# Other places for retention's first tiles, attention values copied out of PSUM, later sigmoids and weight splits, result sums in pieces

## The chip, the cores and the metric

The kernel runs on one NeuronCore of a Trainium2 chip. TensorE (PE) multiplies matrices and writes PSUM, VectorE (DVE), ScalarE (ACT) and GpSimd (POOL) work on tiles, and DMA queues move data between the chip's memory and the on-chip SBUF. SyncE (SP) issues most of the DMAs, GpSimd a few. Every engine works through its own instructions in the order in which they stand, and waits where an operand or the place of a result is not free. The metric is the device time of one execution in microseconds. Lower is better.

## The reference, cut to what matters

One decoder block on a sequence of 1024 tokens with 1024 channels, all in float32. The change touches the two token mixers that run in parallel, retention and dilated attention, and the gates that merge them.

```python
def step(state, inp):              # retention: 4 heads, dk 256, dv 512, 8 chunks of 128
    qi, ki, vi = inp
    s = einsum('bhid,bhjd->bhij', qi, ki) * inner_decay
    o = einsum('bhij,bhje->bhie', s, vi) + einsum('bhid,bhde->bhie', qi, state) * q_decay
    state = state * chunk_decay + einsum('bhjd,bhje->bhde', ki * k_decay, vi)
    return state, o

# token_mixer, after proj = h @ w_in and its split into parts
ro = group_norm(retention(rotary(rq), rotary(rk) * dk ** -0.5, rv))
ret_out = (silu(rg) * ro) @ w_ret_out
for gi, (win, dil) in enumerate(((128, 1), (512, 4), (2048, 16))):   # 4 heads of 128 in each
    o, lse = dilated_group(aq, ak, av, bias, win, dil)   # softmax over a band of keys
att = sum over groups of softmax(lse over groups) * o
att_out = att @ w_att_out
merged = sigmoid(gate_a) * ret_out + sigmoid(gate_b) * att_out
return merged @ w_o
```

Around it stand the modulation by `silu(c) @ w_ada` and the squared-ReLU MLP.

## The kernel before, in words

Float32 products are made of three matmuls on rounded parts: each operand is split into a high part (a cast on ScalarE) and a low part (a subtraction on VectorE), and `mm3` (L197) multiplies low by high, high by low and high by high. A raw weight block of 128x1024 comes in by a DMA on SP's queue and is split by `split_w` (L188). The stages stand in one list of steps. `Steps.run` (L72 to L132) issues the raw loads a few ahead, splits the weights that a step needs, and by default splits those of the next two steps before the body of the step; a step marked manual gets a function `ahead` and calls it where it likes. The order of the work on each engine is the order in which the code issues it; there is no planner. Tiles come from pools in which a new tile waits for the last use of whatever lay in its place.

Values stage (L1072 to L1105): retention's values are projected, modified and stored to the chip's memory in pieces (`vd<-vo`, `vd<-vr`). Then `open_ret` (L517) opens retention's pool over the memory of this stage. Its first tiles are the state and its two parts, and then come the tiles of the chunks.

Retention (`chunk`, L675 to L743): 32 steps g, four heads of eight chunks. A step issues part of the gate projection (rg), the product of keys and values (kv, two halves in two PSUM banks), the scores and key transposes of the next step (`s_kt`: sT, then sm, smh and sml by ScalarE and VectorE, kT, then kh and kl), the state update, the output (o: queries by state, scores by values), the split of the state (stateh, statel), the split of the queries of step g + 2 (`jit_qk`, L608: j, high part on ScalarE and low part on GpSimd), the group norm of o, and the transposes of the last one (`on_T`, L652). `fetch` (L586) brings queries, keys and values three steps ahead. Every step also prepares one modulation block (raw, L455). `u_final` (L663) stores the results of a head (y) to memory.

Result sums (`result_sums`, L574): four blocks of y are added pairwise to t1 to t4 in memory, each by a copying and an adding DMA on GpSimd's queue over all heads. They are issued in the first attention step and are read in the retention output stage (`r_x_load`, L1630).

Attention: two pairs of heads. For each pair `att_step` (L1472) projects keys (ak) and makes scores (sc) and exponentials for six combinations of group and head. Then `cover_step` (L1507 to L1540) runs four gate projections, numbered 0 to 3, in whose course the softmax weights are made (`weights`, L1333), the probabilities are scaled (`pscale`, L1362) and the products with the values are woven in: `pv_tr` (L1380) transposes a bank of probabilities and splits it (pth, ptl), `pv_mm` (L1392) multiplies it by the values (pv), and `pv_end` (L1412) takes the sum out of PSUM: a ScalarE copy for group 0, a VectorE addition to the sum P for groups 1 and 2, and at the end the split of the head's output (ah, al). `v_fetch` and `v_split` (L1291, L1295) bring and split the values (vh, vl). Each gate goes through a sigmoid out of PSUM (L1538) and is stored. Group 2's products run in the step that follows: in the first attention step of the second pair, or for the last pair in `gate_step` (L1557), after which the attention output is projected (ao, `att_out_step`).

## Time and profile before

| | us |
|---|---|
| median of 3 runs | 2228.99 |
| lowest, highest | 2226.23, 2230.13 |
| profiled execution, its own time | 2226.56 |
| its span, first to last instruction | 2224.8 |
| TensorE busy | 2177.1 (98% of the span) |
| VectorE busy | 1454.5 (65%) |
| ScalarE busy | 907.3 (41%) |
| GpSimd busy | 145.5 (7%) |
| mean granted TensorE clock | 0.997 |

Retention's first step stands at about 660 us in the span, the first attention step at about 985, the first pair's cover steps from about 1065, the second pair's from about 1225. A row of a timeline gives start, duration, engine, line, operation, result <- operands, shape, and in brackets the engine's idle time before it with what released it. The granted clock is a share of TensorE's full clock. An average over the span says little here: what a change in one stage is worth is read from that stage's rows.

### The profile page before, as it was taken

Reading aid. Unit: us, or ns where it says so; the run is one execution under the profiler, and the core shown is the slowest. Engines: PE = TensorE matmul, PEld = TensorE weight load, DVE = VectorE, ACT = ScalarE, POOL = GpSimd, SP = SyncE. Lnnn points to the kernel's source line nnn. Section 1 sums busy time; section 2 is a strip of 40 time slices with the busy share of each in tenths; the row PEclk is TensorE's granted clock in tenths of the full one; section 3 lists DMA queues with packets and bytes.
Section 4 is the critical chain, followed back from the end, with each engine's and each line's share of the span. In section 5 each row is a group of like instructions: output and inputs, shape, how many; then the busy total and the mean of one; then the engine's idle time right before and its main releaser. Section 6 shows DMA issues by size and latency. Waiting matters only on the chain.

```text
span 2224.8 us, 27161 instructions
## 1 busy us (share of the span) xinstructions
PE 2177.1 (98%) x10130; PEld 1803.4 (81%) x10130; DVE 1454.5 (65%) x2285; ACT 907.3 (41%) x1665; POOL 145.5 (7%) x168
## 2 busy tenths in 40 slices
PE   7999999999999999999999999999999999999998
PEld 4888888888877888888888788888778888888887
DVE  6628777764448778855554644676876665787855
ACT  4323332223434445544534633424454445533412
POOL 0001111000012122100000000002100000000003
PEclk9999999999999999999999999999999999999999
DMA  9539999725775556549813355645144444745322
GB/s 364 200 134 284 299 284 284 200 103 189 250 268 169 167 179 212 188 162 248 235 60 96 105 196 211 237 160 176 62 149 152 149 156 168 261 139 171 122 85 77
DMA packets 154371, 408.93 MB, mean 184 GB/s; under 512 B 27062, under 2 KB 54973, under 8 KB 149822
## 3 DMA queue, kind: packets, MB, share of 16 engines
q1 hardware_dynamic: 148542, 363.14, 46.5%
q0 software_dynamic: 5696, 44.04, 8.4%
q8 instruction: 80, 1.31, 0.2%
q14 instruction: 53, 0.43, 0.1%
HBM read 316.27 MB, written 156.13 MB: 212 GB/s over the span
## 4 chain that ended last, share of the span: by engine, by line
PE 86%; DVE 6%; ACT 3%; DMA 2%; issue 1%; POOL 0%; SPq 0%; POOLq 0%; DVEq 0%; ACTq 0%
PE qap L203 5%; PE qap L201 5%; PE qap L205 5%; PE av L769 4%; PE fp L203 4%; PE fp L201 4%; PE fp L205 4%; PE rg L201 2%; PE rg L203 2%; PE rg L205 2%; PE f2a L203 2%; PE f2a L201 2%; PE f2a L205 2%; PE ak L201 2%; PE ak L203 2%; PE ak L205 2%
## 5 line engine op out<-in xcount | busy, mean ns | idle before, releaser
L201 PE MATMUL qap<-hh,qaw 128*128 128x512 f32 x216 | 84.0, 389 | 0.0
L203 PE MATMUL qap<-hl,qaw 128*128 128x512 f32 x216 | 84.0, 389 | 0.0
L205 PE MATMUL qap<-hh,qaw 128*128 128x512 f32 x216 | 84.0, 389 | 0.0
L616 POOL TENSOR_TENSOR j<-qk,j 128x512 fp32r<-128x512 f32 x32 | 43.3, 1352 | 465.0 <-ACT j L615 465.0
L1918 ACT ACTIVATE a<-a 128x512 f32<-128x512 f32 x48 | 30.3, 632 | 76.2 <-DVE a L1917 76.2
L1272 ACT ACTIVATE P<-P,ng 128x128 f32<-128x128 f32 (+1 forms) x96 | 41.9, 438 | 39.2 <-DVE ng L1269 39.2
L258 DVE TENSOR_TENSOR fw<-w1r,fw 128x512 fp32r<-128x512 f32 x48 | 33.0, 688 | 37.6 <-ACT fw L248 37.6
L1815 POOL TENSOR_TENSOR accnf<-accnf,sqnf 128x256 f32<-128x256 f32 (+1 forms) x18 | 16.6, 922 | 613.5 <-ACT sqnf L1814 613.4
L258 DVE TENSOR_TENSOR qaw<-wa,qaw 128x512 fp32r<-128x512 f32 x54 | 36.0, 685 | 30.9 <-ACT qaw L248 30.9
L2104 ACT CAST w2h<-w2s 128x512 fp32r<-128x512 f32 x36 | 22.4, 621 | 78.1 <-DVE w2s L2142 77.0
L201 PE MATMUL fp<-h2h,fw 128*128 128x512 f32 x128 | 50.0, 390 | 0.0
L203 PE MATMUL fp<-h2l,fw 128*128 128x512 f32 x128 | 49.8, 389 | 0.0
L205 PE MATMUL fp<-h2h,fw 128*128 128x512 f32 x128 | 49.8, 389 | 0.0
L201 PE MATMUL roa<-rh,rwl 128*128 128x512 f32 x128 | 49.8, 389 | 0.0
L203 PE MATMUL roa<-rl,rwh 128*128 128x512 f32 x128 | 49.8, 389 | 0.0
L205 PE MATMUL roa<-rh,rwh 128*128 128x512 f32 x128 | 49.8, 389 | 0.0
L1653 DVE TENSOR_TENSOR rwl<-rwl,rwh 128x1024 fp32r<-128x1024 f32 x25 | 30.2, 1221 | 29.1 <-ACT rwh L1683 29.1
L638 ACT COPY sm<-sT 128x128 f32<-128x128 f32 x32 | 8.5, 266 | 98.8 <-PE sT L629 92.7
L201 PEld LDWEIGHTS qap<-hh,qaw 128*128 128x128 f32 x216 | 40.5, 188 | 8.5
L205 PEld LDWEIGHTS qap<-hh,qaw 128*128 128x128 f32 x216 | 40.5, 188 | 8.4
L203 PEld LDWEIGHTS qap<-hl,qaw 128*128 128x128 f32 x216 | 40.5, 188 | 8.4
L1815 POOL TENSOR_TENSOR accn<-accn,sqn 128x512 f32<-128x512 f32 x12 | 15.5, 1294 | 478.5 <-ACT sqn L1814 478.5
(3081 smaller groups left out, 7181.0 us busy)
## 6 DMA issues: line engine op xcount, KB each, us to landing
v<-vd SPq DMA_DIRECT2D x32, 512.0 KB, 4.9
raw<-in_w_ada_dram SPq DMA_DIRECT2D x32, 512.0 KB, 4.9
w1r<-in_w_ff_dram SPq DMA_DIRECT2D x32, 512.0 KB, 5.0
vd<-vo SPq DMA_DIRECT2D x24, 512.0 KB, 6.5
yt<-y POOLq DMA_DIRECT2D x6, 2048.0 KB, 15.3
xsd<-as SPq DMA_DIRECT2D x24, 512.0 KB, 2.7
w2r<-in_w_ff2s_dram SPq DMA_DIRECT2D x24, 512.0 KB, 7.6
em<-in_w_ada_dram SPq DMA_DIRECT2D x16, 512.0 KB, 10.2
```

The lines of the kernel that those rows point to most:

```text
L201: nc.tensor.matmul(o, wl, xh, start=first, stop=False, skip_group_check=skip)
L203: nc.tensor.matmul(o, wh, xl, start=False, stop=False, skip_group_check=skip)
L205: nc.tensor.matmul(o, wh, xh, start=False, stop=last, skip_group_check=skip)
L258: nc.vector.tensor_sub(t[:, 512:], src, fv(t[:, :512]))
L616: nc.gpsimd.tensor_sub(t[:, 1], src, fv(t[:, 0]))
L638: nc.scalar.copy(sm, ps[:, :C])
L769: nc.tensor.matmul(av[g][c], x[k][:, c * C:(c + 1) * C], w[j][:, ws], start=k == 0 and (x, j) == parts[0], stop=k == NK - 1 and (x, j) == ...
L1272: nc.scalar.activation(v, v, AF.Exp, bias=ng[:, blk:blk + 1], accum_out=st[:, g, blk, 2 + a:3 + a])
L1653: nc.vector.tensor_sub(lo, fv(lo), fv(hi))
L1815: (nc.vector if f == 7 else nc.gpsimd).tensor_add(G["acc", key], G["acc", key], sq)
L1918: nc.scalar.activation(o, o, AF.Relu)
L2104: nc.scalar.copy(hi, src)
```

## The change: what it does

1. Retention's start. The first split query tile j2, the score tiles and the key tiles of step 0 are allocated first in retention's pool (`chunk_tiles`), the state tiles last, after the fetches for steps 1 and 2 have been issued. In step 0 the state's parts are taken straight out of PSUM, the plain state is copied by ScalarE later, j2 is split before the output instead of after it, and the modulation blocks of steps 0 and 1 are both prepared ahead of step 0.
2. Weights in attention. A step marked "late" gets the preparation of the following two steps as a function and calls it inside its body (`following`).
3. Attention's cover steps. Gates 0 to 2 are copied out of PSUM in halves by VectorE and ScalarE; their sigmoids run in SBUF later, among the value products. `pv_end` copies every product out of PSUM on ScalarE and adds from SBUF. The values of the first group are fetched a step earlier, their high parts are cast before the weights and their low parts taken inside `weights`.
4. Result sums. y and t1 to t4 are tensors for each head, and the sums are 32 transfers of a quarter of the size, issued two in each projection of the attention stage (`with_sums`) and the rest ahead of `gate_step`.

On TensorE the same instructions stand in the same order. VectorE has 5 more, ScalarE 17, GpSimd 24 more (DMA issues); SP's queue has as many, in another order.

```diff
                 issue()
+        def following(s, mine):
+            room = 3 - max(mine, 1)
+            for t in (s + 1, s + 2):
+                if t < len(self.steps) and self.steps[t][2] is True and not self.steps[t][0]:
+                    break
+                if t < len(self.steps) and room > 0:
+                    done = sum(getattr(p, "weight", False) for _, p in self.steps[t][0][:len(results[t])])
+                    prepare(t, room - done, t == s + 2)
+                    room -= weights_of(t)
+                    if len(results[t]) < len(self.steps[t][0]):
+                        break
         pre(issue, lambda room: prepare(0, room), self.marks + [len(flat)])
...
             args = [r for r in results[s] if r is not None]
-            if manual:
+            if manual == "late":
+                body(lambda s=s, mine=mine: following(s, mine), *args)
+            elif manual:
                 body(lambda room=3 - mine, only=False: prepare(s + 1, room, only), *args)
             else:
...
+                following(s, mine)
                 body(*args)
...
         R["p"] = ret_ctx.enter_context(tc.tile_pool(name="ret", bufs=1, reuse_waits="tile"))
-        R["state"] = R["p"].tile([P, 2, DV], F32, name="state")
-        R["sh"] = R["p"].tile([P, 2, DV], F32R, name="stateh")
-        R["sl"] = R["p"].tile([P, 2, DV], F32R, name="statel")
     def etile(name, dt=F32):
         return R["p"].tile([P, 1024], dt, tag="E", bufs=12, name=name)
-    y_d = dram.tile([P, 4, 8, 512], F32, name="y")
-    yt_d = {n: dram.tile([P, 8, 512], F32, name=f"y{n}") for n in ("t1", "t2", "t3", "t4")}
+    y_d = [dram.tile([P, 4, 2, 512], F32, name=f"y{h}") for h in range(H)]
+    yt_d = {n: [dram.tile([P, 2, 512], F32, name=f"y{n}{h}") for h in range(H)] for n in ("t1", "t2", "t3", "t4")}
     YB = ("11", "12", "21", "22")
...
         add(s4, src[1, j])
-    def dma_sum(out, x, y):
...
     def gn_signs():
...
-    def result_sums():
...
+    def sums_of(h):
+        b11, b12, b21, b22 = (y_d[h][:, i] for i in range(4))
+        t1, t2, t3, t4 = (yt_d[n][h] for n in ("t1", "t2", "t3", "t4"))
+        return [(t1, b11, 0), (t1, b12, 1), (t2, t1, 0), (t2, b22, 1), (t4, t2, 0), (t4, b21, 1), (t3, b12, 0),
+                (t3, b22, 1)]
+    sums_left = []
+    def result_sum():
+        if sums_left:
+            out, x, add = sums_left.pop(0)
+            out, x = (t.rearrange("p a b -> p (a b)") for t in (out, x))
+            if add:
+                nc.gpsimd.dma_start(out, x, accum_op=ALU.add, max_dma_last_dim=8192)
+            else:
+                nc.gpsimd.dma_start(out, x)
+    def with_sums(gen):
+        return at(at(gen, 1, result_sum), 5, result_sum)
     hd = {}
...
         if i > 1:
-            t = R["p"].tile([P, 2, 4, C], F32R, tag="j", bufs=2, name=f"j{i}")
+            t = R.pop("j", None)
+            if t is None:
+                t = R["p"].tile([P, 2, 4, C], F32R, tag="j", bufs=2, name=f"j{i}")
         else:
...
         hd["j", i] = t
+    def chunk_tiles():
+        p = R["p"]
+        R["j"] = p.tile([P, 2, 4, C], F32R, tag="j", bufs=2, name="j2")
+        R["sm"] = p.tile([P, C], F32, tag="sm", bufs=1, name="sm00")
+        for n in ("smh", "sml"):
+            R[n] = p.tile([P, C], F32R, tag=n, bufs=2, name=n + "00")
+        for n in ("kh", "kl"):
+            R[n] = p.tile([P, 2, P], F32R, tag=n, bufs=1, name=n + "00")
     def s_kt(i):
...
                 nc.tensor.transpose(pk[:, i, :], hd["qk", g][:, 2 + i], ident)
-        sm = p.tile([P, C], F32, tag="sm", bufs=1, name=f"sm{h}{c}")
-        smh = p.tile([P, C], F32R, tag="smh", bufs=2, name=f"smh{h}{c}")
-        sml = p.tile([P, C], F32R, tag="sml", bufs=2, name=f"sml{h}{c}")
+        if g == 0:
+            sm, smh, sml = R["sm"], R["smh"], R["sml"]
+        else:
+            sm = p.tile([P, C], F32, tag="sm", bufs=1, name=f"sm{h}{c}")
+            smh = p.tile([P, C], F32R, tag="smh", bufs=2, name=f"smh{h}{c}")
+            sml = p.tile([P, C], F32R, tag="sml", bufs=2, name=f"sml{h}{c}")
         nc.scalar.copy(sm, ps[:, :C])
...
             kd = ct[:, CS_KDEC + h:CS_KDEC + h + 1]
-            kh = p.tile([P, 2, P], F32R, tag="kh", bufs=1, name=f"kh{h}{c}")
-            kl = p.tile([P, 2, P], F32R, tag="kl", bufs=1, name=f"kl{h}{c}")
+            if g == 0:
+                kh, kl = R["kh"], R["kl"]
+            else:
+                kh = p.tile([P, 2, P], F32R, tag="kh", bufs=1, name=f"kh{h}{c}")
+                kl = p.tile([P, 2, P], F32R, tag="kl", bufs=1, name=f"kl{h}{c}")
             nc.scalar.mul(kh, pk, kd)
...
             nc.vector.tensor_mul(t, t, hd["srg", h, e])
-            nc.sync.dma_start(y_d[:, 2 * (i % 2):2 * (i % 2) + 2, i // 2], t.rearrange("p (t x) -> p t x", t=2))
+            nc.sync.dma_start(y_d[h][:, 2 * (i % 2):2 * (i % 2) + 2, e // 2], t.rearrange("p (t x) -> p t x", t=2))
     def chunk(h, c, ahead, w=None):
...
         for i, kv in enumerate(kvs):
-            if c == 0:
+            if g == 0:
+                nc.scalar.copy(sh[:, i, :], kv)
+                nc.vector.tensor_sub(sl[:, i, :], kv, fv(sh[:, i, :]))
+            elif c == 0:
                 nc.vector.tensor_copy(st[:, i, :], kv)
...
                                                op0=ALU.mult, op1=ALU.add)
-        if g > 0:
-            ahead(2)
+        if g == 0:
+            jit_qk(2)
+        ahead(2)
         if 0 < g < NG - 1:
...
         mm3([po], hd["s", g], [(vh, vl)], c == 0, True)
-        if c < NC - 1:
+        for i in range(2) if g == 0 else ():
+            nc.scalar.copy(st[:, i, :], kvs[i])
+        if g > 0 and c < NC - 1:
             for i in range(2):
...
                 nc.vector.tensor_sub(sl[:, i, :], st[:, i, :], fv(sh[:, i, :]))
-        if g + 2 < NG:
+        if 0 < g < NG - 2:
             jit_qk(g + 2)
...
         hd["o", h, c] = on
-        if g == 0:
-            ahead(2)
         if c % 2 == 1:
...
         open_ret()
+        chunk_tiles()
         for g in (1, 2):
             fetch(g)
+        R["state"] = R["p"].tile([P, 2, DV], F32, name="state")
+        R["sh"] = R["p"].tile([P, 2, DV], F32R, name="stateh")
+        R["sl"] = R["p"].tile([P, 2, DV], F32R, name="statel")
         banks(False)
...
             steps.add((lambda h, c: lambda ahead, *w: chunk(h, c, ahead, *w))(h, c),
-                      ([wsplit(io["w_rg"][4 * h + c // 2])] if c % 2 == 0 else []) + [mod_load(later_mods[8 * h + c])],
+                      ([wsplit(io["w_rg"][4 * h + c // 2])] if c % 2 == 0 else []) +
+                      [mod_load(later_mods[8 * h + i]) for i in ({0: (0, 1), 1: ()}.get(8 * h + c, (c,)))],
                       manual=True)
...
             nc.sync.dma_start(fv(lo).rearrange("p (a b) -> p a b", a=4), v_rows(pair, g, j))
-    def v_split(pair, g):
+    def v_split(pair, g, low=True):
         for j in range(2):
...
             nc.scalar.copy(hi, fv(lo))
-            nc.vector.tensor_sub(lo, fv(lo), fv(hi))
             A["v", g, j] = (hi, lo)
+            if low:
+                v_low_part(g, j)
+    def v_low_part(g, j):
+        hi, lo = A["v", g, j]
+        nc.vector.tensor_sub(lo, fv(lo), fv(hi))
     def vblk(g, blk, a, i):
...
         nc.scalar.activation(wt, wt, AF.Exp)
+        for j in range(2):
+            v_low_part(0, j)
         for g in range(3):
...
         else:
+            t = A["P", g, a][:, :1024]
+            nc.scalar.copy(t, f)
             r = 4 * g
             sv = sumt.rearrange("p (i r) -> p r i", r=r)
-            nc.vector.tensor_add(sv, f.rearrange("p (r i) -> p r i", r=r), sv)
+            nc.vector.tensor_add(sv, t.rearrange("p (r i) -> p r i", r=r), sv)
         if g == 2:
...
             ps = ps_mm(f"ak{pair}{i}")
-            gen = proj_gen(ps, args[-1])
-            if i == len(combos) - 1:
+            gen = with_sums(proj_gen(ps, args[-1]))
+            if i == len(combos) - 2:
                 v_fetch(pair, 0)
...
                 u_final(H - 1)
-                result_sums()
+                for h in range(H):
+                    sums_left.extend(sums_of(h))
                 open_att()
...
             else:
-                weave_pv(at(gen, 0, lambda: v_split(0, 2)), NK - 1, 0, 2)
+                weave_pv(at(at(gen, 0, lambda: v_split(0, 2)), 5, args[0]), NK - 1, 0, 2)
             if i == 0:
...
             ps = ps_mm(f"gate0{i}")
-            gen = proj_gen(ps, args[-1])
+            gen = with_sums(proj_gen(ps, args[-1]))
             if n == 0:
...
                 drain(gen)
+                v_split(pair, 0, False)
                 scores_end(pair, *combos[-1])
...
             elif n == 1:
-                drain(at(gen, 4, lambda: v_split(pair, 0)))
+                drain(gen)
             elif n == 2:
                 v_fetch(pair, 2)
-                gen = at(gen, 3, lambda: (args[0](3), v_split(pair, 1)))
+                gen = at(at(gen, 3, lambda: (args[0](3), v_split(pair, 1))), 5, sigmoids)
                 weave_pv(gen, NK - 1, pair, 0)
...
             else:
-                weave_pv(at(gen, 3, lambda: [pscale(2, a) for a in range(2)]), NK - 1, pair, 1)
+                gen = at(at(at(gen, 3, lambda: [pscale(2, a) for a in range(2)]), 5, args[0]), 6, sigmoids)
+                weave_pv(gen, NK - 1, pair, 1)
             if n > 1:
...
                 t = ring(f"g0{i}s", F32)
-            nc.scalar.activation(t, flat(ps), AF.Sigmoid)
+            if n < 3:
+                nc.vector.tensor_copy(t[:, :512], ps[:, 0])
+                nc.scalar.copy(t[:, 512:], ps[:, 1])
+                raw_gates.append((i, t))
+            else:
+                nc.scalar.activation(t, flat(ps), AF.Sigmoid)
+                nc.sync.dma_start(gate_d[i], t)
+        return body
+    raw_gates = []
+    def sigmoids():
+        while raw_gates:
+            i, t = raw_gates.pop(0)
+            nc.scalar.activation(t, t, AF.Sigmoid)
             nc.sync.dma_start(gate_d[i], t)
-        return body
     for pair in range(2):
...
                       ([(aq_d[pair, *combos[i - 1]], q_prep(pair, *combos[i - 1]))] if i > 0 else []),
-                      manual=i == pair == 0)
+                      manual=("late" if pair else True) if i == 0 else False)
         for n in range(len(COVER[pair])):
             more = [(aq_d[pair, *combos[-1]], q_prep(pair, *combos[-1]))] if n == 0 else []
-            steps.add(cover_step(pair, n), more + [wsplit(io["w_gate"][len(COVER[0]) * pair + n])], manual=n == 2)
+            steps.add(cover_step(pair, n), more + [wsplit(io["w_gate"][len(COVER[0]) * pair + n])], manual={2: True, 3: "late"}.get(n, False))
     G = {}
...
     mh_ctx = ExitStack()
-    def gate_step(w):
+    def gate_step(ahead, w):
+        while sums_left:
+            result_sum()
         ps = ps_mm("gate9")
         gen = at(proj_gen(ps, w), 2, lambda: v_split(1, 2))
-        gen = at(gen, 3, lambda: [pscale(2, a) for a in range(2)])
-        weave_pv(gen, NK - 1, 1, 1, 2)
+        gen = at(at(gen, 3, lambda: [pscale(2, a) for a in range(2)]), 5, ahead)
+        weave_pv(at(gen, 4, sigmoids), NK - 1, 1, 1, 2)
         att_ctx.close()
...
         nc.sync.dma_start(G[b, j], gate_d[8 * b + j])
-    steps.add(gate_step, [wsplit(io["w_gate"][len(COVER[0] + COVER[1])])])
+    steps.add(gate_step, [wsplit(io["w_gate"][len(COVER[0] + COVER[1])])], manual="late")
     def open_mh():
...
         b = RPLAN[n][0]
-        src = y_d[:, YB.index(b)] if b in YB else yt_d[b]
         for m in range(4):
+            h = 2 * c + m // 2
+            src = y_d[h][:, YB.index(b)] if b in YB else yt_d[b][h]
             Q["x", i, m] = mh(f"rl{i}{m}")
-            nc.sync.dma_start(fv(Q["x", i, m]), src[:, 4 * c + m])
+            nc.sync.dma_start(fv(Q["x", i, m]), src[:, m % 2])
     def r_x(i, j):
```

18 lines of the change are left out of this document (removed).

## The prediction

> **What bounds the kernel now.** I read the page first (busy shares, chain), then a table of stretches around the edited stages, then TensorE's waits in the stretches that are not full, and last single rows there.
>
> ```profile
> PE 2177.1 (98%) x10130; PEld 1803.4 (81%) x10130; DVE 1454.5 (65%) x2285; ACT 907.3 (41%) x1665; POOL 145.5 (7%) x168
> PE 86%; DVE 6%; ACT 3%; DMA 2%; issue 1%; POOL 0%; SPq 0%; POOLq 0%; DVEq 0%; ACTq 0%
> yt<-y POOLq DMA_DIRECT2D x6, 2048.0 KB, 15.3
> ```
>
> TensorE is busy for 98% of the span and carries most of the chain. Its instructions stand in the same order in both programs, none added and none removed, so the change can only move the roughly 48 us in which TensorE is idle, and the time that it runs at less than its full clock. In the next table the columns are length; busy time of PE, PEld, DVE, ACT and POOL; granted clock; DMA share; GB/s.
>
> ```profile
> 660.00:690.00 30.00, 24.65 (x102) 19.51 (x101) 19.71 (x45) 10.73 (x25) 3.77 (x4) 0.89 0.57 204
> 690.00:1080.00 390.00, 389.57 (x1918) 325.32 (x1916) 281.15 (x557) 185.67 (x473) 61.05 (x66) 1.00 0.63 199
> 1080.00:1140.00 60.00, 54.93 (x334) 46.66 (x334) 34.51 (x55) 30.87 (x50) 0.00 (x0) 1.00 0.48 133
> 1140.00:1205.00 65.00, 65.00 (x345) 55.74 (x345) 31.54 (x35) 26.11 (x71) 0.00 (x0) 1.00 0.18 58
> 1205.00:1300.00 95.00, 89.98 (x518) 76.89 (x517) 57.77 (x103) 49.41 (x103) 0.00 (x0) 1.00 0.38 117
> 664.65:670.00 5.35, 5.35 (x20) 4.52 (x21) 1.10 (x4) 0.94 (x3) 0.00 (x0) 0.68 0.57 198
> 677.59:684.00 6.41, 6.41 (x23) 5.21 (x24) 5.87 (x12) 2.84 (x9) 0.54 (x1) 0.73 0.94 336
> ```
>
> Three stretches have something to win: retention's start (660 to 690: 30 - 24.65 = 5.35 us idle), the first head pair's value products (1080 to 1140: 5.07) and the second pair's (1205 to 1300: 5.02). Between them TensorE is full. After retention's idle time the clock falls too: (1 - 0.68) x 5.35 = 1.7 us and (1 - 0.73) x 6.41 = 1.7 us are lost while TensorE works. In both attention stretches the clock stays at 1.00.
>
> TensorE's waits there (total, times, longest), first retention's start, then the three largest lines of pair 0 (pair 1 has the same sizes):
>
> ```profile
> PE kv L201 <- DVE kl L649: 2.2, 1, 2.2
> PE o L201 <- DVE state L705: 1.5, 1, 1.5
> PE kT L634 <- DVE onm L735: 0.9, 1, 0.9
> PE sT L627 <- POOL j L616: 0.7, 1, 0.7
> ```
> ```profile
> PE pv L1408 <- DVE P L1421: 1.7, 2, 0.9
> PE pv L1409 <- DVE ptl010(0, 0, 0)_9158 L1389: 1.2, 1, 1.2
> PE gate L201 <- ACT g00s L1538: 0.8, 1, 0.8
> ```
>
> **Part 1, retention's start.** These rows show why chunk 0 begins late, and what the new order will wait for:
>
> ```profile
> 662.46 0.27 ACT L638 COPY sm<-sT 128x128 f32<-128x128 f32 x1 [6.13 <-DMA vd<-vr]
> 664.65 0.54 PE L201 MATMUL kv<-v,kl 128*128 128x512 f32 x1 [2.21 <-DVE kl L649]
> 670.17 1.28 DVE L703 COPY state<-kv 128x512 f32<-128x512 f32 x2
> 670.88 1.22 ACT L719 CAST stateh<-state 128x512 fp32r<-128x512 f32 x2 [1.15 <-DVE state L703]
> 671.11 0.39 PE L201 MATMUL kv<-v,kl 128*128 128x512 f32 x1
> 672.00 0.61 ACT L615 CAST j<-qk 128x512 fp32r<-128x512 f32 x1
> ```
> ```profile
> qk<-qkd SPq DMA_DIRECT2D x1, 256.0 KB, 7.7
> ```
> ```profile
> 658.00:660.00 2.00, 2.00 (x12) 1.65 (x11) 0.00 (x0) 0.00 (x0) 0.00 (x0) 1.00 1.11 399
> ```
>
> ScalarE's copy of the scores idles 6.13 us because its tile lies where a value tile is still being stored. The new order gives the score and key tiles other memory, and the state tiles take the one that is free last. So the first kv follows at once on the gate projection: the 2.21 us go, and with them the first fall of the clock.
>
> Next in line is the second half of chunk 1's kv: its bank is free only when ScalarE has copied kv00 to the state. On ScalarE stand ahead of it two stateh casts (1.22 for two) and the cast of j2, which is now moved ahead and needs its 256 KB. Their fetch is issued at 658.05 in the trace and lands 7.7 us later, 665.75. In the new SP order one more 512 KB load stands ahead; at the 399 GB/s of that stretch that is 1.3 us: 667.05. Then the cast 0.61 and one state copy about 0.6 (a half of the 1.22): 668.3. TensorE gets there so: from the first kv (664.65) to this matmul (671.11) are 6.46 us, of which the clock lost 1.7, so 4.75; from 662.44 that is 667.2. A new wait of 1.1 us; I add 0.4 for two more hand-overs after it (the state's update before o01, j2's difference on POOL). Bounds: 0 (j2 lands in time) to 3.5 plus a clock fall of 1.7.
>
> The other waits go because VectorE is relieved: the state copies (1.28) go to ScalarE, which idles there, and the modulation's pass over 128x1024 elements that stands just ahead of the state update (1.22, as kl's of that size below) moves to the values stage, where I take it as covered by TensorE; without that cover it would cost at most the same 1.22. The 0.95 before kT goes with them. Sum of part 1: 5.35 + 1.7 + 1.7 = 8.8 lost before, 1.5 after: gain 7.3, between 3.6 and 8.8.
>
> **Part 2, attention's value products, once per pair.**
>
> ```profile
> 1077.61 0.89 ACT L1369 ACTIVATE P<-P,wt 128x256 f32<-128x256 f32 x2
> 1078.52 1.28 ACT L1538 ACT_TABLE_LOAD   x1
> 1079.82 1.02 ACT L1538 ACTIVATE g00s<-gate 128x1024 f32<-128x1024 f32 x1
> 1093.16 1.01 ACT L1417 COPY P<-pv 128x1024 f32<-128x1024 f32 x1
> 1095.03 0.59 ACT L1388 CAST pth001(4, 1, 4)_9062<-pt001(4, 1, 4)_9057 128x512 fp32r<-128x512 f32 x1 [0.86 <-PE pt001(4, 1, 4)_9057 L1384]
> 1097.46 0.48 ACT L1388 CAST pth001(6, 1, 6)_9083<-pt001(6, 1, 6)_9079 128x384 fp32r<-128x384 f32 x1 [1.84 <-PE pt001(6, 1, 6)_9079 L1384]
> 1098.99 0.28 PE L1408 MATMUL pv<-pth001(6, 1, 6)_9083,vl 128*128 128x256 f32 x1
> 1141.89 2.24 DVE L1421 TENSOR_TENSOR P<-pv,P 128x1024 f32<-128x1024 f32 x1 [0.71 <-PE pv L1410]
> 1144.16 1.05 ACT L1426 CAST ah<-P 128x1024 fp32r<-128x1024 f32 x1 [4.24 <-DVE P L1421]
> 1146.39 1.22 DVE L1219 TENSOR_TENSOR kl<-ak,kh 128x1024 fp32r<-128x1024 f32 x1
> 1146.98 1.04 ACT L191 CAST raw_9340h<-raw 128x1024 fp32r<-128x1024 f32 x1
> 1148.57 0.28 PE L201 MATMUL sc<-kh,ql 128*128 128x256 f32 x1
> ```
>
> Gone: the gate's wait (0.8: instead of a table load and a sigmoid, two half copies of about 0.6 free the bank), the wait for ptl010 (1.2: the next weight's splits move behind the casts), the two waits for the sum P (1.7: a copy of 1.01 on ScalarE frees the bank instead of an addition of 2.24 on VectorE), and what is left of the stretch, 1.4 us in small waits for casts and for the values' low part, whose splits move into ScalarE's and VectorE's idle time around the softmax weights. That is all of the 5.07 and 5.02.
>
> New, first: the sigmoids with their table load (1.28 + 1.02 + about 0.95 = 3.25) now stand after pth001(4)'s cast, where ScalarE idles only 1.84. pth001(6) comes 3.25 - 1.84 = 1.4 later; TensorE wants it with a margin of 1098.99 - 1097.94 = 1.05 for the high part, and I estimate 0.5 for the low one behind it, made from the high one: a stall of 0.8 to 0.9.
>
> New, second: the copies are steps in a chain that had none. Behind the last product stand now copy 1.01, addition 2.2, ah 1.05, kh 1.0, kl 1.2, and the copy itself is queued on ScalarE behind ah of the other head, qh and the next raw cast (1.04 each), which in the trace come after. In the trace the keys' low part ends at 1147.61 and the scores want it at 1148.57 (slack 1.0). One copy (1.1 with its hand-over) and two casts of 1.04 ahead of it make 3.2 later, so 2.2 of stall; TensorE itself arrives some 2 to 4 us earlier, but the chain's start moves with it, so 2.4. Bounds 0 (the chain starts as much earlier as it is longer) to 4.
>
> In pair 1 the same chain ends at the gate's last sigmoid and the attention projection:
>
> ```profile
> 1292.45 1.02 ACT L1566 ACTIVATE g<-gate 128x1024 f32<-128x1024 f32 x1
> 1294.60 0.62 PE L201 MATMUL ao<-ah,raw_9954l 128*128 128x512 f32 x2
> ```
>
> The second output's first matmul at 1294.60 wants the bank of this gate, done at 1293.47: slack 1.1; the same 3.3 of copy and casts ahead give 2.2, and 0.2 for the weight of the projection, which is split later.
>
> Net: pair 0 5.07 - 0.8 - 2.4 = 1.9; pair 1 5.02 - 0.8 - 2.2 - 0.2 = 1.8; together 3.7. Does a stall of 2.2 to 2.4 us trip the clock? One of 2.21 did (664.65, then 0.68), while between 1080 and 1300 stalls of up to 1.2 didn't. Two falls would be 3.4 us, none 0; I take one, 1.7. Part 2: gain 2.0, from 10.1 - 1.8 - 8 - 3.4 = -3.1 (two stalls of 4, with falls) to 10.1.
>
> The Trainium skill says under "TensorE: Matmul & The Clock Gate" (Part 1, the HAM clock gate) that the clock falls to half after at least one idle window of about 3.4 us. The trace differs, since a single idle of 2.21 us was followed by 0.68. By the page none of the new stalls costs clock, and the sum would be 1.7 better, 2218.0, inside the forecast's own range below.
>
> The Trainium skill's page "ScalarE: Activation LUTs" ("What ACT_TABLE_LOAD costs") counts 2.66 us for a switch of tables, a drain of 1.38 beside the load of 1.28. That speaks against moving the load between two casts that TensorE waits for: each pair's sigmoids would stall 1.4 more, a gain of 2.8 less, 2222.5, inside that range too. The trace shows the load of 1.28 alone, 0.02 after an activation and 0.02 before the next.
>
> **Part 3, the result sums.** Eight transfers of 2 MB (15.3 each) on POOL's queue become 32 of 512 KB, issued step by step through the attention stage. The bytes are the same; POOL does nothing else from 1080 to 1300 (0.00), and the readers come after 1300. In the trace they ran at a DMA share of 0.63 on average before 1080 without a wait of TensorE (389.57 of 390). Price 0; if a chain of copies and additions in one queue, 32 of some 4 us (a quarter of 15.3), were stretched past its readers, it would cost what it is late, at most a few us. The shifted order on SP's queue I also put at 0: each fetch that comes later was landed over 1 us ahead, and what came nearest, the first transfers of retention, is priced in part 1.
>
> **The sum.** 7.3 + 2.0 = 9.3 us less than the profiled execution's 2226.56: 2217.3. The median of the runs is 2228.99, 2.4 above that execution, so 2219.7 is the forecast beside the median. About 0.2%, 4.5 us, is what a measurement of this kernel can tell from no change.
>
> **Rivals.**
> - All covers hold: no wait of over 0.5 in attention, no fall of the clock, 1 us in retention. For it: VectorE is at 34.51 of 60 there and ScalarE at 30.87, so there is room. Against it: the chain behind the last product is serial, room doesn't shorten it. Gain 8.8 - 1.0 and 10.1 - 2.0, together 15.9: 2213.1.
> - Attention gives nothing or a little less, with both falls and 3 us stalls, and j2's transfer is late by 1 us with a fall: 8.8 - 2.5 - 1.7 = 4.6 and 10.1 - 1.8 - 6 - 3.4 = -1.1: 3.5 better, within what can be told: 2225.5.
> - Slower: ScalarE's queue in attention. Copies, casts, sigmoids and the late weights' splits stand in one strict order, and each waits for a TensorE result of its own; where one is late, all wait. The place is the copy after each of the eight value products beyond the first group. Lost is 1 us for each us that a copy waits longer than the addition did. It decides from about 14 us (9.3 + 4.5), some 1.7 at each of eight, or 7 at each pair's end; for it speaks that the next weight's split (1.04 + 1.22 of such a pass) is now behind the casts, and a late weight stops a whole projection; against it, ScalarE's idle gaps of 1.84 and 4.24 in these rows. At 18 us: 2238.
> - The edit does nothing at retention, since the state's tiles wait for the same store: the first kv still can't be held by them, as it reads keys and values only. I give this no chance of its own beyond the second case.
>
> **Chances and range.** Forecast 0.50 (2215 to 2223), all covers hold 0.17, nearly nothing 0.16, slower 0.17. Faster 0.67, same 0.16, slower 0.17. The range 2211 to 2231 leaves out the worse part of the slower case (0.14) and the best of the second (0.04).
>
> **What would show it.** In the profile after: ScalarE's first copy of the scores at about 658 to 659 rather than 662.46, kv right behind the gate projection, a wait of 1 to 2 us of kv for a state copy, clock at 1.00 from 662 to 690; in attention no wait for P, gate or ptl010, a wait of about 0.8 for pth001(6) or ptl001(6), one of about 2.4 for kl before the first scores of pair 1, and one of about 2.2 at the second attention output. The forecast is wrong if TensorE's idle time in 1080 to 1300 is not below 10, if a raw weight appears as a releaser of TensorE, or if TensorE waits for the sums after 1300.

## The result, and the profile after

The changed kernel takes 2219.0 us (median of 5 runs, 2217.35 to 2219.43), the kernel before 2227.02 (5 runs of the same comparison, 2226.23 to 2230.13). The ratio is 0.9963, with a 95% interval from 0.9952 to 0.9974: 8 us faster, more than the 0.2% that a measurement can tell. The profiled execution has a span of 2217.1 us against 2224.8, 7.7 less. Two executions of over 4500 us, one each of the kernels with whole sums and with the old places below, belong to a slow state and are left out of every median and ratio here.

The same view of stretches as before, now of the changed kernel (length; busy time of PE, PEld, DVE, ACT and POOL; granted clock; DMA share; GB/s), and the kernel before for the one stretch that is cut differently here:

```profile
660.00:690.00 30.00, 28.64 (x137) 22.89 (x135) 21.71 (x48) 14.02 (x32) 5.67 (x6) 1.00 0.69 242
690.00:1205.00 515.00, 511.19 (x2609) 429.72 (x2608) 349.59 (x646) 250.08 (x602) 74.49 (x88) 1.00 0.59 176
1205.00:1300.00 95.00, 90.42 (x505) 76.87 (x504) 60.37 (x105) 53.67 (x105) 0.00 (x0) 0.98 0.37 121
1286.00:1290.00 4.00, 4.00 (x13) 3.12 (x12) 0.95 (x1) 0.00 (x0) 0.00 (x0) 0.57 0.98 356
```
```profile
690.00:1205.00 515.00, 509.50 (x2594) 427.73 (x2593) 347.21 (x646) 242.65 (x593) 61.05 (x66) 1.00 0.56 174
```

In retention's start TensorE's idle time fell from 5.35 to 1.36 us, and the clock, which had cost 3.4 us there, stays at 1.00: 7.4 us. Up to the end of the first pair of heads the idle time fell from 515 - 509.50 = 5.50 to 515 - 511.19 = 3.81: 1.7. In the second pair it fell from 5.02 to 4.58 only, and the clock fell once, to 0.57 over 4 us, which costs (1 - 0.57) x 4 = 1.7: 1.3 worse. The three together make 7.8 of the 7.7 in the spans.

TensorE's waits in the changed kernel (total, times, longest): retention's start, the longest four of pair 0, the longest two of pair 1.

```profile
PE kv L207 <- DVE kl L680: 0.6, 1, 0.6
PE kv L207 <- ACT state L753: 0.6, 1, 0.6
...
PE sc L209 <- DVE kl L1259: 1.1, 1, 1.1
PE pv L1457 <- DVE ptl011(6, 0, 6)_9329 L1437: 0.8, 1, 0.8
PE sc L207 <- ACT kh L1258: 0.5, 1, 0.5
...
PE ao L207 <- ACT g L1636: 1.8, 1, 1.8
PE pt120(0, 0, 0)_10683 L1432 <- DVE P L1415: 1.3, 1, 1.3
```

The waits for the sum P, for the gate, for ptl010 and for vl are gone. In their place stand the keys before pair 1's scores (0.5 + 1.1) and the last gate (1.8), which had been forecast, and two that had not: ptl011(6) and pt120.

### The profile page after: what moved, and what is told of

It reads as the page before. It is cut to its first block, busy times and chain, and to the rows that moved or that the text cites. A ratio compares the mean times of both kernels' runs of the same rounds, so it can differ in the third digit from the quotient of the medians.

```text
span 2217.1 us, 27237 instructions
## 1 busy us (share of the span) xinstructions
PE 2175.5 (98%) x10130; PEld 1802.5 (81%) x10130; DVE 1458.5 (66%) x2289; ACT 919.4 (41%) x1681; POOL 160.8 (7%) x192
```

## The experiments

Each was timed in five rounds beside the kernel before on the same chip, except the one for the clock (one round). They come from four sets of runs, in which the median of the kernel before was 2227.02, 2226.34, 2226.77 and 2226.54, so between sets the ratios compare better than the medians.

| kernel | median | ratio to before, 95% interval |
|---|---|---|
| changed | 2219.0 | 0.9963 [0.9952, 0.9974] |
| part 1 alone | 2221.85 | 0.9979 [0.9971, 0.9988] |
| all but part 1 | 2226.31 | 0.9996 [0.9987, 1.0005] |
| changed, whole sums | 2231.36 | 1.0027 [1.0016, 1.0037] |
| before, sums in pieces | 2226.8 | 0.9998 [0.9989, 1.0007] |
| changed, whole sums, values late | 2225.95 | 0.9996 [0.9987, 1.0005] |
| changed, old places | 2224.82 | 0.9993 [0.9984, 1.0002] |
| changed, state first | 2219.32 | 0.9971 [0.9959, 0.9983] |
| changed, no PSUM copies | 2217.64 | 0.9962 [0.9950, 0.9975] |
| changed, other end of the last step | 2217.52 | 0.9958 [0.9945, 0.9970] |
| changed, copies in group 1 alone | 2216.13 | 0.9948 [0.9935, 0.9962] |
| changed, extra copies for the clock | 2244.54 | 1.0079 [1.006, 1.0097] |

### Part 1 alone, and all but part 1

The first is the kernel before with every edit to `chunk_tiles`, `jit_qk`, `s_kt`, `chunk`, `open_ret` and the modulation loads; the second is the changed kernel without them.

> The kernel before with part 1 alone (places of the first tiles, the state taken out of PSUM, j2 and the modulation earlier). Theory, by parts: retention's start brings nearly all of the 8 us, since between 660 and 690 the idle time fell from 5.35 to 1.36 and the lost clock from 3.4 to 0; so 7.0 to 7.8 us less than before, and two waits of about 0.6 left there. Rival, attention brings most: at most 4 us less. Rival, the earlier first step only hands the gain to a later wait: TensorE idle after 690 grows by over 1 us and the gain is under 6.

> The changed kernel with part 1 undone; parts 2 to 4 alone. Theory, by parts: pair 0 gains 1.7 of idle time, pair 1 gains 0.4 of idle time and loses about 1.7 of clock, the sums nothing: 0 to 1 us less than before. Rival, the attention parts bring 3 us or more and retention less than 5: 3 us less or better. Should the clock not fall in pair 1 this time, it is 2 us less.

Part 1 alone is 2221.85 against 2226.34, 4.5 us faster; all but part 1 is 2226.31, no difference. The second goes with the theory by parts. The first does not in size: 4.5 lies 2.5 under the 7.0 to 7.8 expected, and just above the 4 at which the first rival would hold; the second rival's "under 6" is met, but not its cause, since TensorE's idle time after 690 did not grow (5.38 us up to 1205 against 5.50). Its profile (retention, then the first pair) says why:

```profile
655.00:690.00 35.00, 33.17 (x159) 26.67 (x158) 23.58 (x52) 15.56 (x36) 5.63 (x6) 1.00 0.76 267
1066.00:1145.00 79.00, 73.97 (x422) 62.43 (x421) 47.02 (x80) 40.20 (x68) 0.64 (x1) 0.98 0.47 132
```

Retention's start does lose only 1.83 us and no clock, so 7.0 are gained there in this execution. But the first pair, which stands as it was in code and waits, now has a clock of 0.98 over 79 us, 1.6 us that the profile of before doesn't lose. So a gain may be given back by the clock in a later stage whose waits haven't changed. The fall came about 2.5 us after a wait of 0.90, the last ahead of it, where the kernel before has the same wait (0.88) and keeps its clock:

```profile
1132.05 0.30 PE L1431 MATMUL pv<-pth021(0, 0, 0)_9390,vl 128*128 128x128 f32 x1 [0.90 <-DVE P L1444]
1134.50:1138.50 4.00, 4.00 (x14) 3.24 (x14) 2.32 (x2) 1.04 (x1) 0.00 (x0) 0.57 0.00 0
```

Whether that is so in most executions is not known from one profile. The gains also don't add up: 4.5 alone and nothing alone make 8 together. In the profile of all but part 1 the clock again has a share: pair 0's idle time falls as in the changed kernel, but the granted clock from 660 to 690, in code that it shares with the kernel before, is 0.83 instead of 0.89, about 1.4 us more lost of the 24.5 in which TensorE is busy there. That the clock explains the whole difference is not shown.

### What in part 1 did it: two orders of places

First, the state's tiles in front of the others, all else kept:

```diff
         open_ret()
+        R["state"], R["sh"], R["sl"] = ...   # the three tiles, as before
         chunk_tiles()
         for g in (1, 2):
             fetch(g)
-        R["state"], R["sh"], R["sl"] = ...
```

> The changed kernel with the state's three tiles allocated first again, so that the score and key tiles of chunk 0 lie farther up; everything else of part 1 kept. Theory, the place is the cause of the first wait: the score or key tiles lie over stored value tiles again, ScalarE's first copy of the scores idles some 4 to 6 us for that store, TensorE waits some 2 us for kl before the first kv and its clock falls by about 1.7: 3 to 6 us slower than the changed kernel. Rival, the moved state copies and modulation are the cause: within 1 us of the changed kernel.

That theory fell: 2219.32, like the changed kernel. The score tiles did not wait for a store, though the state stood ahead of them, and the fetch for j2 did wait. That fits tiles that still lie below the stored values, being allocated ahead of the fetched ones, which then got the late places; the addresses themselves no trace shows. ScalarE's rows, then TensorE's wait, then SP's issue of the queries for j2:

```profile
658.23 0.27 ACT L666 COPY sm<-sT 128x128 f32<-128x128 f32 x1 [1.78 <-PE sT L654]
...
668.32 0.62 ACT L630 CAST j<-qk 128x512 fp32r<-128x512 f32 x1 [1.37 <-DMA qk<-qkd]
```
```profile
669.48 0.50 PE L207 MATMUL kv<-v,kl 128*128 128x512 f32 x1 [1.96 <-ACT state L753]
```
```profile
665.20 0.53 SPq L610 DMA_DIRECT2D qk<-qkd  x1
```

The fetch that the changed kernel issues at 657.76 is issued at 665.20, j2 waits for it, the state copies stand behind j2 on ScalarE, and kv's second half waits 1.96 instead of 0.58. So this run shows the wait that the forecast had at that place. It did not cost a fall of the clock.

Second, the old order, score and key tiles behind the fetched ones:

```diff
         open_ret()
-        chunk_tiles()
+        R["state"], R["sh"], R["sl"] = ...
         for g in (1, 2):
             fetch(g)
-        R["state"], R["sh"], R["sl"] = ...
+        chunk_tiles()                        # with j2 last in it
```

> The changed kernel with the tiles of retention's start in the order of before (state, fetched tiles, then score and key tiles, j2); the moved state copies, j2 and the modulation are kept. Theory: it is the score tiles' place over a value tile that is still being stored that made ScalarE idle 6.1 us: this comes back (ScalarE's first copy of the scores after 662), TensorE waits over 2 us for kl before the first kv, and the clock falls once: 3 to 5 us slower than the changed kernel. Rival: with the copies moved, the place costs nothing: within 1.5 us of the changed kernel.

2224.82, 6 us above the changed kernel's 2219.0 with intervals that don't overlap: the place of the score and key tiles (j2's moved with them) carries most of part 1. Its two rows, ScalarE and TensorE's waits:

```profile
663.78 0.27 ACT L666 COPY sm<-sT 128x128 f32<-128x128 f32 x1 [7.79 <-DMA vd<-vr]
```
```profile
PE kv L207 <- DVE kl L680: 4.5, 2, 3.9
```

The cost was above the 3 to 5 expected: the store is waited for longer than before (7.79 against 6.13). SP issues two modulation loads ahead of the last stores here, where the kernel before issues one; that this is the reason was not tested.

### The sums: whole and in pieces

> The changed kernel with the eight whole result sums instead of 32 pieces. Theory, the sums are off TensorE's path and cost nothing either way: within 1 us of the changed kernel (8 us less than before), the idle time of TensorE between 970 and 1300 within 0.5 of that of the changed kernel. Rival, the large transfers hold up the loads of attention now that less slack is left: slower than the changed kernel by over 1.5 us, with a DMA as the releaser of a wait. Rival, the pieces delay attention's loads: faster by over 1.5 us.

```diff
-            gen = with_sums(proj_gen(ps, args[-1]))
+            gen = proj_gen(ps, args[-1])
...
-                for h in range(H):
-                    sums_left.extend(sums_of(h))
+                result_sums()                # with dma_sum, y and yt as before
```

> The kernel before with the result sums in 32 pieces and nothing else. Theory: the pieces only matter once the values are fetched a step earlier; alone they change nothing: within 1.5 us of before, TensorE's waits between 1060 and 1300 as before. Rival: smaller transfers speed up the statistics' round trip through memory for the kernel before as well: 2 us or more faster.

The second run has the same lines turned round, in the kernel before. The pieces alone change nothing (2226.8 against 2226.54). The changed kernel without them takes 2231.36: 12 us slower than with them and slower than before. Neither the theory nor the second rival held; the first rival was nearest. In pair 0 (1066 to 1145) TensorE idles 10.3 us there instead of 3.5, and the clock falls as well: at 0.62 from 1080 to 1088 it costs (1 - 0.62) x 6.61 = 2.5 us of TensorE's busy time. TensorE's two longest waits in pair 0 there, then SP's rows of that kernel, of the changed kernel, and of the kernel before with pieces:

```profile
PE pt000(0, 0, 0)_8939 L1422 <- DVE P L1405: 6.5, 1, 6.5
PE gate L207 <- ACT g00s L1583: 2.3, 1, 2.3
```
```profile
1039.90 0.33 SPq L1365 DMA_DIRECT2D std<-st  x1
1054.55 0.36 SPq L1366 DMA_DIRECT2D stn<-std  x1
1055.01 6.75 SPq L85 DMA_DIRECT2D raw<-in_w_gate_dram  x2
```
```profile
1040.30 0.33 SPq L1375 DMA_DIRECT2D std<-st  x1
1041.73 0.36 SPq L1376 DMA_DIRECT2D stn<-std  x1
1042.52 1.48 SPq L85 DMA_DIRECT2D raw<-in_w_gate_dram  x2
```
```profile
1047.41 0.33 SPq L1340 DMA_DIRECT2D std<-st  x1
1053.54 0.38 SPq L1341 DMA_DIRECT2D stn<-std  x1
```

The softmax statistics go through memory: std is written, then read back as stn, and SP's queue waits with the read until the write has landed. With whole sums the write of 1039.90 lets SP go on only at 1054.55, 14.65 us later; in the changed kernel after 1.43. The size of the pieces is not what decides: in the kernel before with pieces it takes 6.13. What goes with it is how busy the DMA engines are in between. Their mean share is 0.90 in the 14.65 us and 0.74 in the 6.13; the changed kernel's write falls between two pieces, one landed and the next issued at 1041.48:

```profile
1040.30:1041.73 1.43, 1.43 (x8) 1.16 (x7) 0.47 (x1) 1.43 (x2) 0.79 (x2) 1.00 0.08 12
```

The gate's weight is behind it in SP's queue, is waited for on ScalarE (9.63 us, up to 1065.06), and the probabilities behind that cast on VectorE and ScalarE come late.

```profile
1065.06 1.05 ACT L197 CAST raw_8607h<-raw 128x1024 fp32r<-128x1024 f32 x1 [9.63 <-DMA raw<-in_w_gate_dram]
```

The kernel before had a round trip of 10.16 us (1048.07 to 1058.23, at a DMA share of 1.01) and no wait of TensorE from it; so the pieces did shorten it there, by 4 us, and won nothing, since nothing on TensorE's path waited for it. To see what changed, the next run took the whole sums and undid the early fetch and split of the first group's values as well:

```diff
-            if i == len(combos) - 2:
+            if i == len(combos) - 1:
                 v_fetch(pair, 0)
...
-                v_split(pair, 0, False)
...
-                drain(gen)
+                drain(at(gen, 4, lambda: v_split(pair, 0)))
...
-        for j in range(2):
-            v_low_part(0, j)
```

> The changed kernel with whole result sums, as in an earlier run, and besides with the first group's values fetched and split where they were before. Theory: the 1 MB of values ahead of the statistics' store and the gate's weight on SP's queue is what the whole sums collide with; without it the gate's weight comes in time, the wait of 6.5 us for the first scaled probabilities goes, and the time is 8 us or more below that run's: 2219 to 2224. Rival: the whole sums delay the statistics by themselves: the wait of 6.5 stays, 2230 or more.

2225.95: 5 us better than with the early fetch, not the 8 expected, and 2 above the range. SP's rows and TensorE's longest wait in pair 0:

```profile
1040.95 0.33 SPq L1365 DMA_DIRECT2D std<-st  x1
1051.33 0.38 SPq L1366 DMA_DIRECT2D stn<-std  x1
1051.80 1.06 SPq L85 DMA_DIRECT2D raw<-in_w_gate_dram  x2
```
```profile
PE pv L1444 <- ACT pth000(0, 0, 0)_8944 L1424: 2.3, 1, 2.3
```

The round trip is back at 10.4 us (DMA share 1.02), the weight is issued 3.2 us earlier, and the wait of 6.5 is gone, as the theory said. What it did not see: with the values split late, their low parts (2.35 us on VectorE) stand ahead of VectorE's half copy of gate 1, ScalarE's half waits 2.26 for that, and pth000, which stands behind it, makes TensorE wait 2.3 us in each pair. So the parts lean on each other: with whole sums the early values cost 5 us, and with early values the pieces are worth 12. The changed kernel with pieces and late values was not run, so that the pieces pay only with early values is shown for the kernel before alone.

### The products' copies out of PSUM

> The changed kernel with the sums of groups 1 and 2 added straight from PSUM again, all else as changed. Theory: the waits of the value products for P come back (two a pair, 0.7 to 0.9 each), and the chains behind the last products get shorter by one ScalarE copy: the wait for kl before pair 1's scores (0.5 + 1.1) and that of the second attention output (1.8) shrink by about 1 us each, and with the latter under 1 us the clock stays at 1.00 there, which gives 1.7 back: net 0 to 2 us faster than the changed kernel. Rival, the copies were needed: 2 to 4 us slower, since the P waits return and the new waits stay. Rival, the clock fall in pair 1 isn't due to the second output's wait: it stays though that wait is under 1 us.

```diff
-            t = A["P", g, a][:, :1024]
-            nc.scalar.copy(t, f)
...
-            nc.vector.tensor_add(sv, t.rearrange("p (r i) -> p r i", r=r), sv)
+            nc.vector.tensor_add(sv, f.rearrange("p (r i) -> p r i", r=r), sv)
```

2217.64, ratio 0.9962: not told apart from the changed kernel, at the upper end of what the theory allowed. Its waits in pair 0 and the last one in pair 1 are these:

```profile
PE pv L1456 <- DVE P L1470: 1.6, 2, 0.9
PE ak L207 <- DVE P L1470: 0.8, 1, 0.8
...
PE ao L207 <- DVE P L1470: 0.8, 1, 0.8
```

The P waits return, and the waits for the keys and the last gate, with the two unforeseen ones, go; the clock stays at 1.00 in this execution. So the copies moved the idle time from the middle of the chain to its end, and won nothing on balance that these runs can tell.

### The end of the last step, and copies for group 1 alone

> The changed kernel with three edits in the last step of attention: the values of group 2 are split at the start of its projection, only one weight is split ahead of the last product, not two, and the very last product is added from PSUM without a copy. Theory: the wait of 1.3 for the scaled probabilities goes (VectorE has split the values before), the second output's wait shrinks from 1.8 to under 0.9, the first output's 0.3 goes, the clock stays at 1.00: 3 to 4.5 us faster than the changed kernel. Rival, the waits only move (values' transfer not landed so early, the second weight late): within 1 us. Rival, the idle time shrinks but the clock falls all the same: 2 us faster.

```diff
-            nc.scalar.copy(t, f)
+            if (pair, g, a) == (1, 2, 1):
+                t = f
+            else:
+                nc.scalar.copy(t, f)
...
-        gen = at(proj_gen(ps, w), 2, lambda: v_split(1, 2))
-        gen = at(at(gen, 3, lambda: [pscale(2, a) for a in range(2)]), 5, ahead)
+        gen = at(proj_gen(ps, w), 0, lambda: v_split(1, 2))
+        gen = at(at(gen, 3, lambda: [pscale(2, a) for a in range(2)]), 5, lambda: ahead(1))
...
-    steps.add(gate_step, ..., manual="late")
+    steps.add(gate_step, ..., manual=True)
```

2217.52: about 1.5 under the changed kernel's median, less than the intervals can tell, and less than the 3 to 4.5 expected. The wait of 1.3 for pt120 and the 0.3 of the first output went. But the second stayed at 1.8 with another releaser:

```profile
PE ao L207 <- DVE P L1475: 1.8, 1, 1.8
PE pv L1457 <- DVE ptl110(2, 0, 2)_10558 L1437: 0.7, 1, 0.7
```

Now the output waits for a bank that the addition out of PSUM holds, and the earlier split of the values delays ptl110 by 0.7. The two were then taken apart: copies for group 1, where they free a bank that TensorE wants soon, and none for group 2, where the chain is serial.

> The changed kernel with the products of group 1 alone copied out of PSUM, those of group 2 added from PSUM as before, and group 2's values of the last pair split at the start of the last projection. Theory: the chains behind the last products lose a ScalarE copy, so the waits for kl (1.1 and 0.5) and for the last gate (1.8) go and waits of about 0.8 to 0.9 for the sum P take their place, while group 1's P waits stay away: 1 to 3 us faster than the changed kernel. Rival: the sums from PSUM hold the banks as long as the copies held the queue: within 1 us of it.

```diff
-            t = A["P", g, a][:, :1024]
-            nc.scalar.copy(t, f)
+            t = f
+            if g == 1:
+                t = A["P", g, a][:, :1024]
+                nc.scalar.copy(t, f)
...
-        gen = at(proj_gen(ps, w), 2, lambda: v_split(1, 2))
+        gen = at(proj_gen(ps, w), 0, lambda: v_split(1, 2))
```

2216.13, ratio 0.9948: the fastest of all, 10.4 us under the kernel before; against the changed kernel (0.9963) the intervals overlap, so that it beats this too is likely and not shown. The stretch of pair 1 has 95 - 91.79 = 3.2 us of idle time and no loss of clock, where the changed kernel had 4.6 and 1.7:

```profile
1205.00:1300.00 95.00, 91.79 (x518) 78.34 (x518) 61.58 (x106) 54.52 (x104) 0.00 (x0) 1.00 0.39 133
```

But its profiled execution loses clock in pair 0 instead (0.98 over 1066 to 1145), again behind a wait of 0.90.

### How long a wait brings the clock down

> The changed kernel with extra copies of the score tile onto itself on ScalarE in eight later chunks of retention, in which TensorE otherwise never waits: 6, 8, 10, 12, 14, 16, 20 and 24 of them (about 0.27 us each, less the slack there), so single waits of growing length, each over 15 us from the next. Theory: a single wait between 1.3 and 1.8 us is enough to bring the clock to half for about 3.4 us afterwards, and waits below 1.2 don't; nearly all longer waits do. Rival, a full 3.4 us of idle time is needed: the granted clock stays at 1.00 after waits of 2 and 3 us. Rival, it depends on where the wait falls, not on its length alone: falls and none mixed among waits of like length.

```diff
         nc.scalar.copy(sm, ps[:, :C])
+        for _ in range({5: 6, 9: 8, 13: 10, 17: 12, 19: 14, 21: 16, 25: 20, 29: 24}.get(g, 0)):
+            nc.scalar.copy(sm, sm)
```

The copies leave the values as they are. TensorE waited for kl in six of the eight chunks, 0.76 to 4.71 us, not in even steps, since the slack of the chunks differs. Four of the rows with the wait in brackets, then the stretch of 4 us after each of these:

```profile
825.90 0.50 PE L207 MATMUL kv<-v,kl 128*128 128x512 f32 x1 [2.08 <-DVE kl L682]
849.16 0.50 PE L207 MATMUL kv<-v,kl 128*128 128x512 f32 x1 [1.16 <-DVE kl L682]
872.56 0.50 PE L207 MATMUL kv<-v,kl 128*128 128x512 f32 x1 [1.30 <-DVE kl L682]
914.68 0.79 PE L207 MATMUL kv<-v,kl 128*128 128x512 f32 x1 [4.71 <-DVE kl L682]
```
```profile
826.00:830.00 4.00, 4.00 (x11) 3.11 (x12) 3.17 (x8) 3.88 (x9) 1.89 (x2) 0.60 0.00 0
849.20:853.20 4.00, 4.00 (x18) 3.31 (x19) 3.17 (x8) 3.95 (x9) 1.90 (x2) 1.00 0.01 2
872.60:876.60 4.00, 4.00 (x18) 3.29 (x19) 3.17 (x8) 2.56 (x7) 1.90 (x2) 1.00 0.24 93
915.00:919.00 4.00, 4.00 (x10) 3.13 (x10) 3.17 (x8) 3.66 (x9) 1.89 (x2) 0.50 0.01 2
```

2.08 us brought the clock down, as did 4.71 and the longest but one, 4.49; 1.16 and 1.30 didn't. The other profiles disagree between these lengths and beyond them. Of nine waits between 1.81 and 1.96 us, in all the profiles up to 1320 us, five were followed by a fall and four were not: 1.85 before the second output was followed by one in the changed kernel, while 1.82 at the same place in the last-step run and 1.96 in the state-first run were not. From 2.08 to 2.35 us four were and one was not, this one in the second pair of the run with whole sums and late values:

```profile
1241.31 0.39 PE L1444 MATMUL pv<-pth100(0, 0, 0)_10293,vl 128*128 128x256 f32 x1 [2.26 <-ACT pth100(0, 0, 0)_10293 L1424]
1241.30:1245.30 4.00, 3.65 (x23) 3.19 (x24) 2.44 (x4) 1.42 (x3) 0.00 (x0) 1.00 0.93 322
```

And in two runs, those with part 1 alone and with copies in group 1 alone, a fall came behind a wait of 0.90. So the third expectation holds: all single waits of 2.95 us and more were followed by a fall, but from 0.9 to 2.3 us the same length does or doesn't bring one, and a wait of 3.4 us is not needed. What decides it there is not shown.

## Why the prediction was right, point by point

**Retention.** Forecast 7.3 us, in the profile 7.4 (4.0 idle, 3.4 clock). The first kv follows at once, the clock stays up, and the new wait for the state copy is there, 0.58 where 1.1 stood. The step "In the new SP order one more 512 KB load stands ahead" was wrong: that load is issued among the stores of the values stage, the queries for j2 at 657.76 as before, and ScalarE had no wait for them:

```profile
666.58 0.62 ACT L630 CAST j<-qk 128x512 fp32r<-128x512 f32 x1
667.11 1.07 ACT L753 COPY state<-kv 128x512 f32<-128x512 f32 x2
```

What queued there was ScalarE's own work, the casts of kh and stateh. The 0.4 added for two more hand-overs came as one of 0.64, at another place: the low keys of chunk 2 stand on VectorE behind a weight's split and a modulation pass of 1.22 each. That the places are the cause was argued by the 6.13 us; the old-places run shows it. These 7.4 are those of one profiled execution; timed alone, part 1 brought 4.5, and leaving it out of the changed kernel cost 7.3.

**Pair 0.** Forecast 1.9, measured 1.7, from other parts. The sigmoids in the gap of 1.84 cost 0.41 (0.20 and 0.21) where 0.8 to 0.9 stood: the low part's margin had been guessed. The chain of copies before the scores cost 1.6 where 2.4 stood. Not seen was the row between:

```profile
1108.01 1.23 DVE L198 TENSOR_TENSOR raw_8634l<-raw,raw_8634h 128x1024 fp32r<-128x1024 f32 x1
1109.14 1.24 DVE L198 TENSOR_TENSOR raw_8741l<-raw,raw_8741h 128x1024 fp32r<-128x1024 f32 x1
1110.28 0.57 DVE L1437 TENSOR_TENSOR ptl011(6, 0, 6)_9329<-pt011(6, 0, 6)_9324,pth011(6, 0, 6)_9328 128x384 fp32r<-128x384 f32 x1
```

The splits that had held up ptl010 were moved and hold up ptl011(6) by 0.76 instead. The prediction counted the wait that went and not who stands behind the moved step.

**Pair 1.** Forecast 1.8 of idle time less one fall of the clock, 1.7; measured 0.44 and 1.7. The wait for the last gate came as said, 1.8 for 2.2. The step that failed is the same kind: the values' split, left at its place, now stands ahead of the scaling, whose transposes wait 1.30. The fall of the clock, taken as one of two possible, was one; that was luck, since waits of 1.8 to 2.0 us went both ways in the runs.

**The Trainium skill's two rules.** On the clock, "TensorE: Matmul & The Clock Gate" (Part 1) has a fall after an idle window of about 3.4 us. Here 2.08 sufficed, 1.85 did in the changed kernel, and two falls followed waits of 0.90. That its window runs free of the kernel, which the same section says, fits that equal waits went both ways. On the table load, "ScalarE: Activation LUTs" ("What ACT_TABLE_LOAD costs") counts a drain of 1.38 beside the load of 1.28; by that, an estimate, TensorE would have stalled 1.4 more behind the late sigmoids. Its stall there was 0.41, and the sigmoid starts 0.02 after the load, so no drain showed here.

**The sums.** Price 0 was right for the whole change, and the reason given, that these transfers had run beside TensorE without a wait, was wrong as a cover: they ran beside a kernel that fetched the values later. "The shifted order on SP's queue I also put at 0" holds only with the pieces; that cover is worth 12 us, and no rival named it. The estimate of 4 us for a piece, a quarter of 15.3, was too low: 24 of them took 7.3 in the median, still in time, as the last is issued at 1143 and TensorE has no wait for them after 1300.

```profile
yt<-y POOLq DMA_DIRECT2D x24, 512.0 KB, 7.3
```

**The rivals.** The slower one, ScalarE's queue, appeared as several waits of 0.5 to 1.8 and stayed far from the 14 us at which it decides. None of the three signs of being wrong appeared: TensorE's idle time from 1080 to 1300 is 220 - 212.32 = 7.7 us, under 10, and the one wait for a raw weight, 0.6 after 1300, stands in both kernels. Where the range leaves out "the best of the second", only the case in which all covers hold can be meant, since no other reaches under 2211. The number was right, 2219.7 against 2219.0, and that it came so close is luck, with two errors that cancelled: attention gave 0.4 where 2.0 stood, and the forecast was set from a median of before 2 us higher than that of the final comparison.

## What to carry to other kernels

Where TensorE's order doesn't change, an edit can be priced from its waits, but each moved step needs the second question: who stands behind it at the new place, on every engine and queue. A part that does nothing alone may be what another part rests on, so leave out one part at a time from the whole, besides trying each alone. A copy out of PSUM takes a wait away where the bank is wanted next and adds one at the end of a serial chain; that the better placing is worth time is likely here, not shown.

## What the runs showed of the hardware that was not expected

The same small write to memory, followed by its read (the last statistics of pair 0), held SP's queue for 1.43 us at a DMA share of 0.08, 6.13 at 0.74, and 10.16 to 14.65 at 0.90 to 1.02. The clock fell to half after single waits of 2.08 and 1.85 us and twice behind one of 0.90, and didn't after others of 1.96 and 2.26; one of the falls behind 0.90 gave back 1.6 us in a stage whose code and waits were unchanged.
